# A two-layer hybrid decoder trunk: convolution inputs turned by VectorE and transfers, state space work and probability transfers placed otherwise

## Chip, core and metric

The kernel runs on one core of one Trainium2 chip. The metric is the device time of one execution in microseconds; three runs of the kernel before gave 1489.04, 1489.55 and 1492.39 us, median 1489.55 us.

## What is computed

Two layers (DEPTH 2) over 256 tokens of 1024 channels, all in float32. In each layer:

```
h += 1/2 * RMSNorm(SwiGLU(RMSNorm(h)))
h +=       RMSNorm(HybridMixer(RMSNorm(h)))
h += 1/2 * RMSNorm(SwiGLU(RMSNorm(h)))
```

The mixer, on which the change acts:

```
q, k, v, z, xbc, dt_raw, u, vg, gate_raw = split(xn @ w_in)
y_a = moba_attention(q, k, v)                  # 8 heads x 128
xbc = silu(causal_depthwise_conv(xbc, conv_w, conv_b))   # 1536 channels, 4 taps along the tokens
xs, bm, cm = split(xbc, [1024, 1280])          # 16 heads x 64; 2 groups of state 128
dt  = softplus(dt_raw + dt_bias);  a = -exp(a_log)
y_s = ssd_scan(xs, dt, a, bm, cm) + d_skip * xs          # chunks of 128 tokens
y_s = rms_norm(y_s * silu(z))
y_c = gelu(u) * (tril(sgu_w) @ layer_norm(gelu(vg)) + sgu_b)
merged = sigmoid(g0)*(y_a @ p_attn) + sigmoid(g1)*(y_s @ p_ssm) + sigmoid(g2)*(y_c @ p_sgu)
return merged @ w_out
```

With 256 tokens attention sees a single block of 256 keys, so it is causal attention with a linear distance penalty.

## The kernel before

The tokens are two tiles of 128 (t = 0, 1). All weights come as 495 blocks of 128 x 1024 float32 (512 KB), streamed in order through three rings. SyncE (SP) loads a block into `raw` (6 buffers, L160); ScalarE (ACT) rounds it into `whi` (L180), VectorE (DVE) writes the rest `wlo = raw - whi` (L181), 11 buffers each (SPLIT). Each product of the projections is three TensorE (PE) matmuls, hi x hi, hi x lo, lo x hi (L213 to L215), over 512 columns. A 512-column projection of the mixer (a chunk) is 4 blocks, so 48 matmuls for both token tiles.

The order of all work is that in which Python writes it. `gemm` walks the blocks; after each block and token tile `pump` advances a program clock by 0.65 us per three matmuls (`tick`) and lets the next block be split. Everything else is in generator tasks: `yield w` lets a task rest until the clock has gone on by `w`; the table `W` names these rests. `finish` runs tasks to their end at once, whatever they still had to rest. Each engine executes its instructions in the order written, and SP its transfers in the order issued: an instruction that waits holds up all that stands behind it on its engine.

The mixer projects in the order xbc (three chunks; the first two together), z (2), q (2), k (2), v (2), then gate and p_ssm (`br`), vg, gate and p_attn, u, gate and p_sgu, w_out. Beside them:

- `conv(c, ps)`, one task for each xbc chunk. ACT scales the projection into `xtok`, token-major (L514). PE turns it into channel-major `xc`: 8 transposes of 128 x 128 (`ctr`, L523), copied from PSUM by ACT (L526). Then ACT writes tap 3 with the bias (L545, four of 256 tokens), DVE adds taps 0 to 2 in two halves of six instructions (L551, a rest `cv` after each), ACT applies Silu (L554), and for chunks 0 and 1 PE turns the result back (`xstr`, L562) and ACT copies it into `xs` (L563). `finish(*cv)` stands behind the z projections (L952).
- `turn_whole` and `land_whole`, until now for q alone: DVE transposes each 32 x 32 square of a token tile in place (L292), 4 transfers of 64 KB for each tile write the squares to DRAM scratch `turnw` (L294), and one transfer of 512 KB brings the whole chunk back turned (L298). `turn` and `land` (L277 to L285) do the same by token tile for k, the probabilities `sc` and `y`.
- `ssd`: for t = 0, 1 and group g = 0, 1 it makes two sets of decay weights (`weights`: a PE matmul `seg` L707, DVE L709, four ACT exponentials L713, DVE L715), with a rest `w1` between and `w2` behind them; then PE multiplies them with the scaled `xs` (`yd`, L738), for t = 1 also the state with C (`yo`, L744), and DVE adds and gates (L741 to L749). `scaled(t)` writes `y = D * xs` on POOL (L695) and scales `xs` by dt on DVE (L698). After each t, `turned` transposes `y` (L277) and sends it through DRAM.
- `attention`: scores (`qk`), softmax, then DVE transposes the probabilities (L277), 8 transfers write them out, after a rest `out` two bring them back (L827), and after a rest `pv` PE multiplies them with v (L837).

Of the kernel before, what the change touches and what calls it, by code (L numbers as in the profile page):

```python
# [16 lines left out]
P = 128  # L17
L = 2
S = 256
# [25 lines left out]
ACC, TR = 5, 3  # L45


W = {'gw': 6.5, 'tr': 0, 'parts': 0, 'sq': 1.3, 'lead': 3.9, 'sq2': 5.2, 'hh': 5.2, 'x0': 0.65, 'cv': 5.2, 'cs': 6.5, 'xs': 0, 'dt1': 2.6, 'dt2': 0, 'dt3': 5.2, 'cb': 2.6, 'w1': 2.6, 'w2': 6.5, 'ys': 3.9, 'qk': 3.9, 'vv': 0, 'qs': 0, 'ex': 0, 'p1': 10.4, 'p2': 0, 'p3': 3.9, 'ge': 0, 'ln': 10.4, 'sv': 0, 'yc': 9.1, 'mg': 3.9, 'pv': 11.7, 'out': 7.8, 'in': 9.1}


@with_exitstack
def trunk(ctx, tc, a):
# [11 lines left out]
    def b4(name, shape=(P, 1024), dt=F32):  # L64
        return big.tile(list(shape), dt, name=name, tag="b4", bufs=B4)
# [49 lines left out]
    def spawn(g, wait=0):  # L115
        e = [g, wait, False]
        tasks.append(e)
        return e
# [35 lines left out]
    raws, parts = {}, {}  # L154
# [38 lines left out]
    lead = [0]  # L193
# [93 lines left out]
    def turn_whole(toks):  # L287

        rd = dram.tile([4, P, S], F32, name="turnw", tag="turnw", bufs=6)
        v = rd.rearrange("k (c i) (t a j) -> t a i (k c) j", c=4, a=4, t=NT)  # L290
        for t in range(NT):
            V.transpose(toks[t], toks[t])  # L292
            for b in range(4):
                nc.sync.dma_start(v[t, b], toks[t][32 * b:32 * b + 32, :].rearrange("p (b j) -> p b j", j=32))  # L294
        return rd
# [192 lines left out]
    def mixer(l, x, r2, nxt):  # L488
        pl = par[:, l, :]
# [28 lines left out]
        def transposed(toks, place, eng):  # L518

            for t in range(NT):  # L520
                ps = tr("ctr")
                for j in range(4):
                    T.transpose(ps[:, j * P:(j + 1) * P], toks[t][:, j * P:(j + 1) * P], ident)  # L523
                p3 = ps.rearrange("p (k t) -> p k t", k=4)
                if eng == "a":
                    A.copy(place(t), p3)  # L526
                else:
                    V.tensor_copy(place(t), p3)
                yield W["tr"]
# [5 lines left out]

        def conv(c, ps):
            toks = tokens(ps, r2, "xtok")
            xc = b4("xc", (P, 4, S))
            yield W["x0"]
            yield from transposed(toks, lambda t: xc[:, :, t * P:(t + 1) * P], "a")  # L540
            o = b4("conv", (P, 4, S))
            w = lambda j, k: pl[:, G_CW + 4 * (4 * c + j) + k:G_CW + 4 * (4 * c + j) + k + 1]
            for j in range(4):
                ct = 4 * c + j
                A.activation(o[:, j, :], xc[:, j, :], AF.Identity, scale=w(j, 3),  # L545
                             bias=pl[:, G_CB + ct:G_CB + ct + 1])
            for jj in (0, 2):
                for k in range(3):
                    s = 3 - k
                    for j in (jj, jj + 1):  # L550
                        V.scalar_tensor_tensor(o[:, j, s:], xc[:, j, :S - s], w(j, k), o[:, j, s:],  # L551
                                               op0=ALU.mult, op1=ALU.add)
                yield W["cv"]
            A.activation(o, o, AF.Silu)  # L554
            yield W["cs"]
            if c < 2:
                for t in range(NT):
                    if t not in xs:
                        xs[t] = b4(f"xs{t}")
                    pt = tr("xstr")  # L560
                    for j in range(4):
                        T.transpose(pt[:, j * P:(j + 1) * P], o[:, j, t * P:(t + 1) * P], ident)  # L562
                    A.copy(xs[t][:, 512 * c:512 * c + 512], pt)  # L563
                    yield W["xs"]
            else:
                bc["T"] = o
                pt = tr("btr")
                for g in range(SG):
                    T.transpose(pt[:, g * P:(g + 1) * P], o[:, g, 0:P], ident)
                bc["b"] = b2("btok", (P, SG * P))  # L570
                A.copy(bc["b"], pt[:, :SG * P])
# [106 lines left out]
        def ssd(ysx, rs):  # L678
# [13 lines left out]
            def scaled(t):  # L692

                y[t] = b4(f"y{t}")
                G.tensor_tensor(h3(y[t]), h3(xs[t]), hpar[:, l, 2, :, None].to_broadcast([P, SH, SP]),  # L695
                                op=ALU.mult)
                xdt[t] = xs[t]
                V.tensor_tensor(h3(xdt[t]), h3(xs[t]),  # L698
                                st["dt"][:, t * SH:(t + 1) * SH, None].to_broadcast([P, SH, SP]), op=ALU.mult)
# [19 lines left out]
            for t in range(NT):  # L719
                for g in range(SG):  # L720
                    weights(t, 2 * g)
                    if g == 0:
                        scaled(t)
                    yield W["w1"]
                    weights(t, 2 * g + 1)
                    if t == 0:

                        pst = tr("state")
                        T.matmul(pst, bc["b"][:, g * P:(g + 1) * P], xw[:, 512 * g:512 * g + 512],
                                 start=True, stop=True)  # L730
                        A.copy(state[:, 512 * g:512 * g + 512], pst)
                    yield W["w2"]
                    c = slice(512 * g, 512 * g + 512)
                    py = tr("yd")
                    for q in (2 * g, 2 * g + 1):
                        for j in range(4):
                            hh = q * 4 + j
                            T.matmul(py[:, (hh - 8 * g) * SP:(hh - 8 * g + 1) * SP], ws[t, q][:, j, :],  # L738
                                     xdt[t][:, hh * SP:(hh + 1) * SP], start=True, stop=True)
                        ws.pop((t, q))  # L740
                    V.tensor_tensor(y[t][:, c], py, y[t][:, c], op=ALU.add)  # L741
                    if t == 1:
                        po = tr("yo")
                        T.matmul(po, cT(g, 1), state[:, c], start=True, stop=True)  # L744
                        tmp = b2("yo")
                        V.tensor_tensor(h3(tmp, 8), h3(po, 8),
                                        st["eac"][:, 8 * g:8 * g + 8, None].to_broadcast([P, 8, SP]), op=ALU.mult)
                        V.tensor_tensor(y[t][:, c], y[t][:, c], tmp, op=ALU.add)
                    V.tensor_tensor(y[t][:, c], y[t][:, c], zs[t][:, c], op=ALU.mult)  # L749
                rs[t] = rsqrt([sumsq(y[t], "sy")], "rs", 1.0 / D)  # L750
                yt[t] = spawn(turned(t, y[t], pl[:, G_SSM:G_SSM + 8]), wait=1.3)


        qk = {}
# [26 lines left out]
        def attention(yax, free):  # L781
            for t in range(NT):
# [36 lines left out]
                for g in range(2):  # L819
# [2 lines left out]
                                    rden[:, None, 4 * g:4 * g + 4, None].to_broadcast([P, 4 * m, 4, 32]), op=ALU.mult)  # L822
                    rd[g] = turn(sc[g], m)
                    yield 1.3
                yield W["out"]
                for g in range(2):
                    land(sc[g].rearrange("p (m e) -> p m e", m=m), rd[g])  # L827
                yield W["pv"]
# [350 lines left out]
```

## Time and profile before

| | |
|---|---|
| median of three runs | 1489.55 us |
| the profiled execution, its own time | 1490.6 us |
| its span, first to last instruction | 1488.8 us |
| mean granted TensorE clock | 0.992 |
| busy: PE, DVE, ACT, POOL | 1461.8, 970.3, 767.7, 55.0 us |
| first matmul of xbc in layer 0 | at 193.2 us |

The two layers repeat each other: what happens in the mixer of layer 0 happens about 736 us later in layer 1 (ACT's first copy into `xs` starts at 246.52 and at 982.48). Times below are those of layer 0 in the profiled execution, in us from the span's start. A PE row's duration includes its way through the array, so rows overlap; what counts is the distance between starts, 0.227 us for a 512-column matmul at full clock.

### The profile page before, as it was taken

The page shows a single profiled execution, that of the slowest core. Times are in us where ns is not written, and L with a number is a line of the kernel's source. Part 1 is how long each engine was busy: PE and PEld are TensorE (multiplying, and loading weights), DVE is VectorE, ACT ScalarE, POOL GpSimd, SP SyncE. Part 2 cuts the span into 40 slices and gives each one's busy share as a digit, 9 for nine tenths or more (in the row PEclk, how much of TensorE's full clock was granted, in tenths as well). Part 3 has the DMA queues.
Part 4 walks back from the last instruction along what each step waited for, and adds up shares of the span by engine and source line. Part 5 has one row for each costly group of instructions (what it writes and reads, how often), then busy time and mean ns, then how long its engine had stood idle before and what let it go on. Part 6 is the DMA issues. An engine that isn't in the chain of part 4 may idle for free. (4 is left out here: it accounts for less than half of the span.)

```text
span 1488.8 us, 18560 instructions
## 1 busy us (share of the span) xinstructions
PE 1461.8 (98%) x6706; PEld 1208.7 (81%) x6706; DVE 970.3 (65%) x1188; ACT 767.7 (52%) x1051; POOL 55.0 (4%) x98
## 2 busy tenths in 40 slices
PE   9999999989989999999999999999899899999998
PEld 7888888778878888888888888888788788888886
DVE  6766477767666857666486564876776677676652
ACT  6544367455454537444364443765463635464541
POOL 0000020000000000000000000200000000000000
PEclk9999999999999999999999999999999999999999
DMA  8978555577567445878568874656774765477760
GB/s 293 332 228 263 185 191 177 161 209 224 198 213 224 172 156 197 282 243 255 154 205 268 253 251 128 221 171 187 227 230 150 230 211 169 132 261 249 262 199 28
DMA packets 151003, 312.23 MB, mean 210 GB/s; under 512 B 35456, under 2 KB 76544, under 8 KB 150912
## 3 DMA queue, kind: packets, MB, share of 16 engines
q1 hardware_dynamic: 150336, 310.73, 64.3%
q8 instruction: 52, 0.85, 0.2%
q10 hardware_dynamic: 576, 0.33, 0.1%
q14 instruction: 39, 0.32, 0.1%
HBM read 288.98 MB, written 22.02 MB: 209 GB/s over the span
## 5 line engine op out<-in xcount | busy, mean ns | idle before, releaser
L181 DVE TENSOR_TENSOR wlo<-raw,whi 128x1024 fp32r<-128x1024 f32 x495 | 593.9, 1222 | 325.9 <-ACT whi L180 323.5
L180 ACT CAST whi<-raw 128x1024 fp32r<-128x1024 f32 x495 | 511.7, 1051 | 394.8 <-PE gu L215 162.9
L213 PE MATMUL gu<-whi,xh 128*128 128x512 f32 x704 | 276.1, 392 | 1.7 <-ACT xh L328 1.3
L214 PE MATMUL gu<-wlo,xh 128*128 128x512 f32 x704 | 274.9, 391 | 0.0
L215 PE MATMUL gu<-whi,xl 128*128 128x512 f32 x704 | 274.8, 390 | 0.0
L213 PEld LDWEIGHTS gu<-whi,xh 128*128 128x128 f32 x704 | 132.6, 188 | 30.2 <-ACT xh L328 1.7
L214 PEld LDWEIGHTS gu<-wlo,xh 128*128 128x128 f32 x704 | 132.6, 188 | 28.0 <-DVE wlo L169 0.9
L215 PEld LDWEIGHTS gu<-whi,xl 128*128 128x128 f32 x704 | 132.6, 188 | 28.1 <-DVE xl L329 0.4
L213 PE MATMUL dn<-whi,hTh 128*128 128x512 f32 x352 | 137.5, 391 | 0.0
L215 PE MATMUL dn<-whi,hTl 128*128 128x512 f32 x352 | 137.0, 389 | 0.0
L214 PE MATMUL dn<-wlo,hTh 128*128 128x512 f32 x352 | 136.9, 389 | 0.0
L215 PEld LDWEIGHTS dn<-whi,hTl 128*128 128x128 f32 x352 | 66.1, 188 | 13.9
L213 PE MATMUL gate<-whi,xh 128*128 128x512 f32 x192 | 77.1, 402 | 0.0
L214 PEld LDWEIGHTS dn<-wlo,hTh 128*128 128x128 f32 x352 | 66.1, 188 | 13.6
L213 PEld LDWEIGHTS dn<-whi,hTh 128*128 128x128 f32 x352 | 66.1, 188 | 13.3
L215 PE MATMUL gate<-whi,xl 128*128 128x512 f32 x192 | 75.4, 393 | 0.0
L214 PE MATMUL gate<-wlo,xh 128*128 128x512 f32 x192 | 75.2, 392 | 0.0
L328 ACT CAST xh<-xg 128x512 fp32r<-128x512 f32 (+1 forms) x25 | 15.1, 603 | 63.0 <-DVE xg L326 63.0
L713 ACT ACTIVATE ssw<-ssw,nacs 128x128 f32<-128x128 f32 x64 | 20.5, 391 | 50.8 <-DVE ssw L709 50.8
L215 PEld LDWEIGHTS gate<-whi,xl 128*128 128x128 f32 x192 | 36.3, 189 | 7.8
L214 PEld LDWEIGHTS gate<-wlo,xh 128*128 128x128 f32 x192 | 36.4, 190 | 6.9
L213 PEld LDWEIGHTS gate<-whi,xh 128*128 128x128 f32 x192 | 36.4, 190 | 6.8
(239 smaller groups left out, 2231.3 us busy)
## 6 DMA issues: line engine op xcount, KB each, us to landing
raw<-in_mix SPq DMA_DIRECT2D x232, 512.0 KB, 4.5
raw<-in_gu SPq DMA_DIRECT2D x175, 512.0 KB, 4.9
raw<-in_dn SPq DMA_DIRECT2D x88, 512.0 KB, 4.5
turn<-hh SPq DMA_DIRECT2D x160, 64.0 KB, 1.8
hh<-turn SPq DMA_DIRECT2D x40, 256.0 KB, 5.2
row_ffn_post_g<-in_ffn_post_g SPq DMA_DIRECT2D x4, 512.0 KB, 5.7
turnw<-qtok SPq DMA_DIRECT2D x32, 64.0 KB, 2.2
qT<-turnw SPq DMA_DIRECT2D x4, 512.0 KB, 5.9
```

Of the source, the lines that this page charges most:

```text
L180: A.copy(hi, w)
L181: V.tensor_tensor(lo, w, hi.bitcast(F32), op=ALU.subtract)
L213: T.matmul(o, xh(k, t), hi[:, off:off + n], start=first, stop=False)
L214: T.matmul(o, xh(k, t), lo[:, off:off + n], start=False, stop=False)
L215: T.matmul(o, xl(k, t), hi[:, off:off + n], start=False, stop=last)
L328: A.copy(o_h, xg)
L713: A.activation(w[:, j, :], w[:, j, :], AF.Exp, bias=st["nacs"][:, c:c + 1])
```

## The change

Five edits, all in the mixer:

- `conv`: chunks 0 and 1 no longer use PE for their first turn. They rest 2.6, go through `turn_whole` (DVE, 16 transfers for both chunks), rest `out` (7.8), are brought back by `land_whole` into `xc`, rest `in` (9.1), and go on as before. Chunk 2 (B and C) keeps PE.
- `ssd`: `scaled(1)` is written in the work of t = 0, g = 1 and no longer in that of t = 1, g = 0.
- the turn of `y` of t = 0 starts 6.5 behind the end of its work, not 1.3.
- `attention`: the rest ahead of the transfers that bring the probabilities back is a new key `so`, 3.9, where it was `out`, 7.8.
- the rest `pv` behind it is 13.0, where it was 11.7.

```diff
-W = {..., 'mg': 3.9, 'pv': 11.7, 'out': 7.8, 'in': 9.1}
+W = {..., 'mg': 3.9, 'so': 3.9, 'pv': 13.0, 'out': 7.8, 'in': 9.1}
...
         def conv(c, ps):
             toks = tokens(ps, r2, "xtok")
-            xc = b4("xc", (P, 4, S))
-            yield W["x0"]
-            yield from transposed(toks, lambda t: xc[:, :, t * P:(t + 1) * P], "a")
+            if c < 2:
+                yield 2.6
+                rd = turn_whole(toks)
+                yield W["out"]
+                xc = b4("xc", (P, 4, S))
+                land_whole(xc, rd)
+                yield W["in"]
+            else:
+                xc = b4("xc", (P, 4, S))
+                yield W["x0"]
+                yield from transposed(toks, lambda t: xc[:, :, t * P:(t + 1) * P], "a")
...
                 for g in range(SG):
                     weights(t, 2 * g)
-                    if g == 0:
-                        scaled(t)
+                    if t == 0:
+                        scaled(g)
                     yield W["w1"]
...
-                yt[t] = spawn(turned(t, y[t], pl[:, G_SSM:G_SSM + 8]), wait=1.3)
+                yt[t] = spawn(turned(t, y[t], pl[:, G_SSM:G_SSM + 8]), wait=1.3 if t else 6.5)
...
-                yield W["out"]
+                yield W["so"]
                 for g in range(2):
                     land(sc[g].rearrange("p (m e) -> p m e", m=m), rd[g])
                 yield W["pv"]
```

Because the program clock orders everything, these edits move other instructions too. The lines of the changed kernel behind `conv` are 8 higher (L545 there is L553, L562 is L570). Three places follow, all in layer 0; layer 1 has the same.

The first place is ACT from the end of the first z chunk to the end of the second. `zs` is Silu of z, `xc`, `conv` and `xs` are those of the convolution. Before:

```order
L526 COPY xc<-ctr 128x4x128 x2
L545 ACTIVATE conv<-xc,par 128x256 x8
L180 CAST whi<-raw 128x1024 x3
...
L554 ACTIVATE conv<-conv 128x1024 x2
L180 CAST whi<-raw 128x1024 x2
L655 ACTIVATE zs_2135<-z,r_1662 128x512
L655 ACTIVATE zs_2137<-z,r_1739 128x512
L180 CAST whi<-raw 128x1024
L563 COPY xs_2164<-xstr 128x512 x2
```

Now:

```order
L663 ACTIVATE zs_2099<-z,r_1662 128x512
L663 ACTIVATE zs_2101<-z,r_1739 128x512
L553 ACTIVATE conv<-xc,par 128x256 x8
L180 CAST whi<-raw 128x1024 x2
L562 ACTIVATE conv<-conv 128x1024
L180 CAST whi<-raw 128x1024 x2
L562 ACTIVATE conv<-conv 128x1024
L571 COPY xs_2206<-xstr 128x512
L571 COPY xs_2213<-xstr 128x512
L562 ACTIVATE conv<-conv 128x1024
L571 COPY xs_2206<-xstr 128x512
```

The eight tap instructions of chunks 0 and 1 stood a chunk and a half ahead of `zs`; now they stand behind it, and the first of the three Silus is chunk 2's. On DVE the order behind them is: six taps of chunk 0, six of chunk 1, three `wlo`, six of chunk 0, six of chunk 1. On PE the sixteen `xstr` transposes, which stood in two groups inside the second z chunk, now stand behind its last matmul:

```order
L213 MATMUL z<-whi,xh_1682 128x512
L214 MATMUL z<-wlo,xh_1682 128x512
L215 MATMUL z<-whi,xl_1683 128x512
L570 MATMUL xstr<-con,conv 128x128 x16
L577 MATMUL btr<-con,conv 128x128 x2
L213 MATMUL q<-whi,xh_1595 128x512
```

so the q projection stands behind all of them.

The second place is DVE in `ssd`, from the gating of t = 0, g = 1 to the second set of weights of t = 1, g = 0 (`seg` are the exponents' sums, `ssw` the weights, `xs` the state space input that `scaled` multiplies). Before:

```order
L749 TENSOR_TENSOR y_2468<-y_2468,zs_2135 128x512
L709 TENSOR_TENSOR ssw<-seg,con 128x512
L715 TENSOR_TENSOR ssw<-ssw,cbt 128x512
L698 TENSOR_TENSOR xs_2189<-xs_2189,dt 128x1024
L277 STREAM_TRANSPOSE qtok<-qtok 128x512 x2
L277 STREAM_TRANSPOSE y_2468<-y_2468 128x1024
L181 TENSOR_TENSOR wlo<-raw,whi 128x1024
L709 TENSOR_TENSOR ssw<-seg,con 128x512
L715 TENSOR_TENSOR ssw<-ssw,cbt 128x512
```

Now:

```order
L757 TENSOR_TENSOR y_2468<-y_2468,zs_2099 128x512
L717 TENSOR_TENSOR ssw<-seg,con 128x512
L723 TENSOR_TENSOR ssw<-ssw,cbt 128x512
L277 STREAM_TRANSPOSE qtok<-qtok 128x512 x2
L181 TENSOR_TENSOR wlo<-raw,whi 128x1024
L717 TENSOR_TENSOR ssw<-seg,con 128x512
L723 TENSOR_TENSOR ssw<-ssw,cbt 128x512
L181 TENSOR_TENSOR wlo<-raw,whi 128x1024 x2
L277 STREAM_TRANSPOSE y_2468<-y_2468 128x1024
```

Two instructions have left the stretch between the two sets of weights: L698 stands a set of weights earlier (in t = 0, g = 1), the transpose of `y` stands behind the second set.

The third place is SP around the probabilities (`sc`) of t = 1, in one piece of the difference:

```order
 L280 DMA turn_128_3532<-sc 32x8x128 x4
 L280 DMA turn_128_3545<-sc 32x8x128 x4
-L160 DMA raw<-in_mix 128x1024 x4
+L160 DMA raw<-in_mix 128x1024 x2
 L285 DMA sc<-turn_128_3532 128x2x512
 L285 DMA sc<-turn_128_3545 128x2x512
-L160 DMA raw<-in_mix 128x1024 x17
+L160 DMA raw<-in_mix 128x1024 x19
```

Two weight loads instead of four stand between writing the probabilities out and bringing them back. On PE the `pv` matmuls of both token tiles stand 18 projection matmuls earlier than before.

## Rows read from the trace of the kernel before

**Rows 1.** The page: from its first part busy time, share of the span and number of instructions of each engine; from its list of groups the cast of the weights on ACT (count, busy us, mean ns of one, idle time ahead and its releaser).

```profile
PE 1461.8 (98%) x6706; PEld 1208.7 (81%) x6706; DVE 970.3 (65%) x1188; ACT 767.7 (52%) x1051; POOL 55.0 (4%) x98
...
L180 ACT CAST whi<-raw 128x1024 fp32r<-128x1024 f32 x495 | 511.7, 1051 | 394.8 <-PE gu L215 162.9
```

**Rows 2.** What PE itself waited for over the whole span, longest first: engine, line and tile, the releaser; us in total, times, longest us.

```profile
PE pv L837 <- DMA sc<-turn: 9.1, 2, 4.6
PE yd L738 <- DVE ssw L715: 7.7, 2, 3.8
```

**Rows 3.** The timeline of PE, from the turn of xbc to the start of q: start, us, engine, line, operation, out<-in, shape, count.

```profile
218.66 1.03 PE L523 MATMUL ctr<-con,xtok 128*128 128x128 f32 x8
...
219.45 0.48 PE L213 MATMUL xbc<-whi,xh 128*128 128x512 f32 x1
...
228.60 0.39 PE L213 MATMUL z<-whi,xh 128*128 128x512 f32 x1
...
252.92 0.39 PE L215 MATMUL z<-whi,xl 128*128 128x512 f32 x1
...
253.28 0.48 PE L213 MATMUL q<-whi,xh 128*128 128x512 f32 x1
```

**Rows 4.** The timeline of ACT in the same stretch; in brackets idle time ahead and its releaser.

```profile
216.35 2.42 ACT L514 ACTIVATE xtok<-xbc,r 128x512 f32<-128x512 f32 x4
...
222.50 4.05 ACT L545 ACTIVATE conv<-xc,par 128x256 f32<-128x256 f32 x8
...
237.34 2.00 ACT L554 ACTIVATE conv<-conv 128x1024 f32<-128x1024 f32 x2
...
241.61 1.25 ACT L655 ACTIVATE zs<-z,r 128x512 f32<-128x512 f32 x2
...
246.52 1.07 ACT L563 COPY xs<-xstr 128x512 f32<-128x512 f32 x2 [2.10 <-PE xstr L562]
```

**Rows 5.** The timeline of DVE in the same stretch.

```profile
221.65 1.22 DVE L181 TENSOR_TENSOR wlo<-raw,whi 128x1024 fp32r<-128x1024 f32 x1 [0.69 <-ACT whi L180]
...
231.38 4.82 DVE L551 SCALAR_TENSOR_TENSOR conv<-xc,par,conv 128x253 f32<-128x253 f32 x12
...
239.61 3.49 DVE L181 TENSOR_TENSOR wlo<-raw,whi 128x1024 fp32r<-128x1024 f32 x3
```

**Rows 6.** The way through DRAM as q takes it: the timeline of DVE and of SP's queue at q's first chunk, then from the page's list of transfers (count, KB each, median us from issue to landing) the weight loads and q's two kinds.

```profile
274.92 1.30 DVE L292 STREAM_TRANSPOSE qtok<-qtok 128x512 f32<-128x512 f32 x2
...
275.65 4.39 SPq L294 DMA_DIRECT2D turnw<-qtok  x8
...
raw<-in_mix SPq DMA_DIRECT2D x232, 512.0 KB, 4.5
...
turnw<-qtok SPq DMA_DIRECT2D x32, 64.0 KB, 2.2
qT<-turnw SPq DMA_DIRECT2D x4, 512.0 KB, 5.9
```

**Rows 7.** The timeline of DVE in `ssd`, between the two sets of weights of t = 1, g = 0, and the last set of t = 1, g = 1.

```profile
310.00 1.26 DVE L715 TENSOR_TENSOR ssw<-ssw,cbt 128x512 f32<-128x512 f32 x1 [1.35 <-ACT ssw L713]
311.19 1.21 DVE L698 TENSOR_TENSOR xs<-xs,dt 128x1024 f32<-128x1024 f32 x1
312.32 1.30 DVE L277 STREAM_TRANSPOSE qtok<-qtok 128x512 f32<-128x512 f32 x2
313.54 1.20 DVE L277 STREAM_TRANSPOSE y<-y 128x1024 f32<-128x1024 f32 x1
314.67 1.18 DVE L181 TENSOR_TENSOR wlo<-raw,whi 128x1024 fp32r<-128x1024 f32 x1
315.77 0.68 DVE L709 TENSOR_TENSOR ssw<-seg,con 128x512 f32<-128x512 f32 x1
317.79 0.69 DVE L715 TENSOR_TENSOR ssw<-ssw,cbt 128x512 f32<-128x512 f32 x1 [1.34 <-ACT ssw L713]
...
332.55 0.69 DVE L715 TENSOR_TENSOR ssw<-ssw,cbt 128x512 f32<-128x512 f32 x1 [1.35 <-ACT ssw L713]
```

**Rows 8.** The timeline of PE in `ssd`, t = 1: the `yd` matmuls of g = 0 in two parts, the first projection matmul behind them, the `yd` of g = 1 and the first projection matmul behind those.

```profile
313.71 1.00 PE L738 MATMUL yd<-xs,ssw 128*128 128x64 f32 x8
...
318.54 1.30 PE L738 MATMUL yd<-xs,ssw 128*128 128x64 f32 x8 [3.83 <-DVE ssw L715]
...
321.88 0.63 PE L213 MATMUL v<-whi,xh 128*128 128x512 f32 x1
...
333.43 1.89 PE L738 MATMUL yd<-xs,ssw 128*128 128x64 f32 x16
...
335.67 0.80 PE L213 MATMUL v<-whi,xh 128*128 128x512 f32 x1
```

**Rows 9.** The 2 us from 319 on: from:to, us, busy time of PE, PEld, DVE, ACT, POOL, the granted clock of TensorE, the busy share of the DMA engines and GB/s.

```profile
319.00:321.00 2.00, 2.00 (x9) 1.42 (x8) 2.00 (x2) 2.00 (x4) 0.00 (x0) 0.58 1.07 202
```

**Rows 10.** The probabilities of t = 1: the timelines of PE, DVE and SP's queue.

```profile
432.60 3.75 PE L837 MATMUL pv<-sc,v 128*128 128x128 f32 x16 [4.42 <-DMA sc<-turn]
...
422.25 4.63 DVE L181 TENSOR_TENSOR wlo<-raw,whi 128x1024 fp32r<-128x1024 f32 x4 [0.25 <-ACT whi L180]
...
418.34 7.77 SPq L160 DMA_DIRECT2D raw<-in_mix  x4
426.22 0.93 SPq L285 DMA_DIRECT2D sc<-turn  x2
```

More of the change, by code (lines that the diff above doesn't have):

```diff
@@ L45 @@
 ACC, TR = 5, 3
-W = {'gw': 6.5, 'tr': 0, 'parts': 0, 'sq': 1.3, 'lead': 3.9, 'sq2': 5.2, 'hh': 5.2, 'x0': 0.65, 'cv': 5.2, 'cs': 6.5, 'xs': 0, 'dt1': 2.6, 'dt2': 0, 'dt3': 5.2, 'cb': 2.6, 'w1': 2.6, 'w2': 6.5, 'ys': 3.9, 'qk': 3.9, 'vv': 0, 'qs': 0, 'ex': 0, 'p1': 10.4, 'p2': 0, 'p3': 3.9, 'ge': 0, 'ln': 10.4, 'sv': 0, 'yc': 9.1, 'mg': 3.9, 'pv': 11.7, 'out': 7.8, 'in': 9.1}
+W = {'gw': 6.5, 'tr': 0, 'parts': 0, 'sq': 1.3, 'lead': 3.9, 'sq2': 5.2, 'hh': 5.2, 'x0': 0.65, 'cv': 5.2, 'cs': 6.5, 'xs': 0, 'dt1': 2.6, 'dt2': 0, 'dt3': 5.2, 'cb': 2.6, 'w1': 2.6, 'w2': 6.5, 'ys': 3.9, 'qk': 3.9, 'vv': 0, 'qs': 0, 'ex': 0, 'p1': 10.4, 'p2': 0, 'p3': 3.9, 'ge': 0, 'ln': 10.4, 'sv': 0, 'yc': 9.1, 'mg': 3.9, 'so': 3.9, 'pv': 13.0, 'out': 7.8, 'in': 9.1}
 @with_exitstack
```

## The prediction

> **What bounds the kernel.** I read the busy times first: PE is busy 98% of the span [rows 1], so the time is PE's work plus PE's waits. Then PE's own waits: two places are worth a name, the `yd` matmuls, which wait for VectorE's decay weights, and the `pv` matmuls, which wait for the probabilities' way back from DRAM; each occurs once in each layer, 7.7 and 9.1 us in all [rows 2]. Then the timelines around each edit, for what ends last there. No other engine is near its limit over the span, so an edit counts only where PE has to wait for it, or where it takes an instruction off PE. All times are layer 0's; layer 1 repeats them, so each term is doubled at the end. About 0.2%, 3 us, is what a measurement of this kernel can tell from no change.
>
> **Term 1, PE's transposes (gain).** Eight `ctr` transposes start at 218.66 and the next matmul at 219.45, 0.79 us on, and that one holds PE 0.08 us longer than the usual 0.227: 0.88 us for eight [rows 3]. Sixteen leave: 1.76 us. The first z matmul then starts at 228.60 - 1.76 = 226.84. The sixteen `xstr` move behind z, so the last z matmul (252.92 before) is over at about 253.15 - 1.76 - 1.75 = 249.65.
>
> The Trainium skill prices this otherwise: "TensorE: Matmul & The Clock Gate", section "Part 4: PE-mode transpose", gives some 275 ns for one transpose in a kernel's context, by which sixteen would be worth 4.4 us. The trace does not agree as to what they displace: eight of them hold the next matmul up by 0.88 us.
>
> **Term 2, the convolution's chain (loss).** The transposes that leave PE were cheap, and what replaces them is late. Follow the new order.
>
> Transfers: `xtok` is done at 218.77 [rows 4]. DVE transposes four tiles at 1.30 for two [rows 6] behind two `wlo`, of which the second (221.65, 1.22 long [rows 5]) comes some 0.7 earlier without ACT's copies between: done at about 224.8. SP then needs 4.39 for eight writes, so 8.8 for sixteen, from about 222.8 to 231.6; +2.2 to land: 233.8 [rows 6]. A return of 512 KB lands in 5.9 [rows 6]: 239.7 for chunk 0. The second is issued behind it; it lands between 0.4 (SP's issue) and 5.9 later, 240.1 to 245.6.
>
> ACT: the taps L553 stand behind both `zs`. Those start at 241.61 - 1.76 = 239.85 and take 1.25 [rows 4], so chunk 0's taps start at 241.1 even though its input may be there sooner; eight take 4.05: chunk 1's start at 243.1, all end at 245.15. Two `whi`, 1.05 each [rows 1], 2.0 as a pair, to 247.15, Silu of chunk 2 (two in 2.00 [rows 4]) to 248.15, the next `whi` to 249.15.
>
> DVE: six taps take 2.41 (twelve in 4.82 [rows 5]). Chunk 0 from 241.7 to 244.1, chunk 1 to 246.5; three `wlo` (3.49 for three [rows 5]), whose third waits for the `whi` that ends at 249.15: 250.4. Then chunk 0's second half to 252.8, chunk 1's to 255.2.
>
> PE: Silu of chunk 0 ends at 253.9, and PE, finished with z at 249.65, stands still for 4.3 us. First eight `xstr`, ACT's two copies (1.07 [rows 4]), Silu of chunk 1 to 256.55, eight more `xstr` and two `btr`: q starts at 257.6, where it started at 253.28 [rows 3]. So the chain costs **4.3 us net of term 1**. A further price comes behind a standstill: after the 3.83 us wait for `yd` the granted clock was 0.58 over the two microseconds from 319 on [rows 9], between the chip's two levels, 1.2 and 2.4 GHz. 4.3 is longer than 3.83, so I count the `xstr` at half clock, 0.8 us each eight, of which the first eight's half delays the copies: 1.1. Taken: **+5.4**. Ends: +4.3 (clock stays up) and +8.2 (transfers 2.8 late, because three weight loads stand ahead of the returns on SP, at 4.5 each when alone [rows 6]).
>
> What hides the rest: DVE's 2.6 us of transposes fall where it has idle time, and SP's 8.8 us delay weight loads that are up to eleven blocks of 12 matmuls, 2.7 us each, ahead of PE; without that lead it would be up to 8.8. ACT stands still ahead of its taps under the same cover.
>
> **Term 3, the state space work (gain).** Before, DVE does between the two sets of weights of t = 1, g = 0: L698 1.21, two transposes of k, the transpose of `y` 1.20, one `wlo` [rows 7]. PE has its first `yd` done at 314.7 and waits to 318.54 [rows 8]. Without L698 (1.13 from start to start) and `y` (1.13), and with the first L715 no longer stretched to 1.26 from 0.69 (POOL's L695, which ran in that moment, goes with L698), DVE would be 2.8 earlier; L698 now stands one set of weights earlier, where DVE has up to 1.4 idle, and leaves 0.4 of its 1.2 behind. So PE waits to about 316.15: 1.45 instead of 3.83, too short for what happened to the clock. Before, the row of work from 318.54 to the next projection matmul at 321.88 took 3.34; at full clock it is 1.7 (g = 1 took 2.24 for both halves of `yd` and `yo` [rows 8], less 0.85 for one half, plus 0.3 for a score matmul). The projection would go on at 317.85, 4.0 earlier.
>
> But not all of it is kept. PE then reaches the last `yd` at 317.85 + 11.1 = 328.95, its second half at 329.8. The weights for that were ready at 333.24 before (L715 at 332.55 [rows 7]). DVE's chain to there is 2.3 earlier at its start, takes in the moved transpose of `y` (1.2), and fills 0.8 of its waits for ACT with it: 331.35. So a new wait of 1.5 us arises at the last `yd`, and the next projection matmul starts at 331.35 + 1.4 = 332.75, where it started at 335.67: **-2.9**, taken -2.8. Ends: -5.4 (no wait left at either `yd`) and 0 (all given back at the last one).
>
> The later turn of y of t = 0 has nothing behind it before the p_ssm projection: nothing. On SP its return stands behind two weight loads and ahead of the second k; k's lead there covers it.
>
> **Term 4, the probabilities.** At t = 0 nothing waited before, and the returns are issued two loads sooner against 4.1 us (18 matmuls) less on PE: nothing, at worst +1. At t = 1 PE comes 4.1 us earlier, at 424.1 instead of 428.2 (432.60 - 4.42 [rows 10]). SP: of the four loads (from 418.34 to 426.11) the first goes at once and the second needs the first of the four `wlo` that start at 422.25, over at 423.4 [rows 10]; with two loads ahead the returns are issued at about 423.8, not 426.22. The first `pv` followed its return's issue by 6.4 before, with three loads just ahead of it; q's single return takes 5.9 and a weight load 4.5 [rows 6], so I take 5.0 with one load ahead: 428.8. PE waits 4.7 where it waited 4.4. The end of the stage moves by +0.3, and DVE's chain ahead is a little shorter, since one cast there no longer stands behind a wait for PE. Taken: **0**, ends -1 and +1.7.
>
> **Sum.** +5.4 - 2.8 + 0 = +2.6 a layer, +5.2 for two. Against the profiled execution's own 1490.6 us (its span is 1488.8) that is 1495.8; that execution is 1.05 above the median, so the median should come to **1494.8 us**.
>
> **Rivals.**
> 1. The transfers are the late part, not the chain (18%). For it: 16 writes of 128-byte pieces and three loads ahead of the returns; against it: ACT is not ready before 241.1. At +8.2 a layer: +5.4 x 2 = +10.8, 1500.4; with `pv` at +1.7 too, 1503.8.
> 2. The terms cancel (25%): term 2 at its lower end, 4.3, and term 3 at -4.3 because the last `yd` loses little: 1489.6. If instead the transposes were worth their whole rows, which the trace speaks against, term 1 would gain 2.6 more a layer: 1489.6 as well. The second way has 4 of the 25. The price in the Trainium skill's "TensorE: Matmul & The Clock Gate", section "Part 4: PE-mode transpose", comes to the same time.
> 3. Faster (15%): moving L698 and `y` off DVE clears both `yd` waits with their half clock, -5.4 in layer 0 and no less in layer 1, against term 2 at 4.3 with the clock up: -1.1 a layer, and with `pv` at its -1 end, since the same two microseconds bring DVE's softmax forward, -2.1: 1485.4. It decides at the last `yd` of t = 1: the weights must be there by 329.8. Against it: two microseconds of DVE work are moved there, not removed.
>
> The forecast itself, slower by 3 to 9 us, has 42%. So faster 0.15, same 0.25, slower 0.60. The range, 1486 to 1504, reaches from rival 3's better half to rival 1's worse end; the forecast's own is 1492.5 to 1498.5.
>
> **What would show it.** In the changed profile: PE waits at `xstr` for ACT's Silu, about 4 us and then 1 to 2 us, in both layers, with the granted clock at half behind it; q starts 4 to 6 us later relative to the first xbc matmul. The taps L553 of chunk 0 start right behind `zs`: if they start later and wait for the transfer, rival 1 is at work. The 3.8 us waits at `yd` fall to some 1.5, and a new one stands at the last `yd`. `pv` still waits some 4 to 5 us. No wait at `xstr`, or one under 2 us, would make the prediction wrong; so would a `pv` wait that is gone.

## The result

The changed kernel takes 1505.67 us in the median (1503.93 to 1507.45, four runs) where the kernel before, run beside it, takes 1489.78: a ratio of **1.0104, interval 1.0092 to 1.0116**, by that ratio 15.5 us slower. Forecast were 1494.8 us, range 1486 to 1504. The profiled execution is the slowest of the four (1507.45 us); it has a span of 1505.6 us (1488.8 before) and a mean granted clock of 0.988 (0.992 before, 0.989 to 0.991 in the other three). The direction was right, the size a third of what came.

### The profile page after: what moved, and what is told of

It reads as the page before. It is cut to its first block, busy times and chain, and to the rows that moved or that the text cites. A ratio compares the mean times of both kernels' runs of the same rounds, so it can differ in the third digit from the quotient of the medians.

```text
span 1505.6 us, 18548 instructions
## 1 busy us (share of the span) xinstructions
PE 1465.2 (97%) x6674; PEld 1209.5 (80%) x6674; DVE 972.4 (65%) x1196; ACT 765.1 (51%) x1043; POOL 55.7 (4%) x98
## 4 chain that ended last, share of the span: by engine, by line
PE 79%; DVE 11%; ACT 4%; issue 3%; DMA 2%; POOL 0%; SPq 0%; DVEq 0%; ACTq 0%; POOLq 0%
PE gu L213 10%; PE gu L214 10%; PE gu L215 10%; PE dn L213 5%; PE dn L215 5%; PE dn L214 5%; DVE wlo L181 5%; PE br L213 3%; PE br L215 3%; PE br L214 3%; PE xbc L213 1%; PE xbc L215 1%; PE xbc L214 1%; ACT whi L180 1%; DVE conv L559 1%
```

## The profile after

The waits of PE over the span, columns as in [rows 2]:

```profile
PE xstr L570 <- ACT conv L562: 14.3, 4, 5.5
PE pv L845 <- DMA sc<-turn: 8.2, 2, 4.1
PE yd L746 <- DVE ssw L723: 4.6, 4, 1.4
PE br L213 <- ACT ysh L682: 3.1, 2, 1.6
```

Two rows are new: `xstr`, which was forecast, and `br`, which was not. Where the time went is read by following the same instructions in both traces: the start in the changed kernel minus the start before, and how it grows from one landmark to the next (us; the landmarks are the last matmul of the feed-forward layer ahead, the last of q, the first of the gate behind v, the first of vg, the first of u).

| stretch | forecast | layer 0 | layer 1 |
|---|---|---|---|
| xbc to last q: terms 1 and 2 | +5.4 | +9.27 | +9.20 |
| to the first gate: `yd`, term 3 | -2.8 | -1.29 | -2.30 |
| to vg: p_ssm | 0 | +1.95 | +2.16 |
| to u: `pv` of t = 1, term 4 | 0 | -1.72 | -0.56 |
| sum | +2.6 | +8.21 | +8.50 |

16.7 us together, of 16.8 by the spans. The convolution is more than all of it. PE there, to be held against [rows 3]:

```profile
249.24 0.39 PE L215 MATMUL z<-whi,xl 128*128 128x512 f32 x1
255.17 1.97 PE L570 MATMUL xstr<-con,conv 128*128 128x128 f32 x8 [5.54 <-ACT conv L562]
258.77 1.97 PE L570 MATMUL xstr<-con,conv 128*128 128x128 f32 x8 [1.63 <-ACT conv L562]
```

What PE waited for stands in the chain of work that ended last, followed back through this stretch (start, us, what):

```profile
238.52 0.24 PE z L215
...
238.79 1.06 ACT whi L180
...
239.88 1.22 DVE wlo L181
241.10 1.65 DVE conv L559 x5
242.75 0.24 issue
242.99 2.12 DVE conv L559 x6
...
245.36 2.12 DVE conv L559 x6
...
247.72 0.47 DVE conv L559
248.20 3.40 DVE wlo L181 x3
251.60 2.38 DVE conv L559 x6
...
254.06 1.07 ACT conv L562
...
255.17 1.98 PE xstr L570 x8
```

From 239.88 to 254.06 it is DVE: a `wlo` (whose cast on ACT had waited for PE), 18 taps, three `wlo`, six taps. No transfer is in it. ACT's taps and SP's queue in layer 0, and ACT's taps in layer 1:

```profile
240.95 4.05 ACT L553 ACTIVATE conv<-xc,par 128x256 f32<-128x256 f32 x8
...
222.75 10.08 SPq L294 DMA_DIRECT2D turnw<-xtok  x16
232.93 1.40 SPq L160 DMA_DIRECT2D raw<-in_mix  x3
234.42 1.06 SPq L298 DMA_DIRECT2D xc<-turnw  x2
...
986.09 4.05 ACT L553 ACTIVATE conv<-xc,par 128x256 f32<-128x256 f32 x8 [0.93 <-DMA xc<-turnw]
```

In layer 0 the taps follow `zs` at once, but without a margin: their return was issued at 234.42 and took 6.5 us to land. In layer 1 they wait 0.93 us for it, and the stage is no longer for that. Behind the standstill the clock, columns as in [rows 9]:

```profile
253.00:255.00 2.00, 0.00 (x0) 0.00 (x0) 2.00 (x6) 0.94 (x1) 0.00 (x0) 0.76 0.89 332
255.00:257.00 2.00, 1.83 (x8) 1.57 (x8) 2.00 (x5) 0.70 (x2) 0.00 (x0) 0.50 0.17 70
...
261.00:263.00 2.00, 2.00 (x6) 1.61 (x6) 0.00 (x0) 1.81 (x4) 2.00 (x2) 0.50 0.00 0
263.00:265.00 2.00, 2.00 (x22) 1.65 (x22) 0.00 (x0) 0.00 (x0) 1.35 (x1) 0.68 0.00 0
```

Half clock, 1.2 GHz, holds from about 254 to 264: through both groups of `xstr` and into q.

## Experiments

All ratios are to the kernel before, run beside; "stage" is the first row of the table above, measured in that run's trace.

**The edit alone, and all but it.** `e_conv_only` has the other four edits undone, `e_no_conv` the block `if c < 2` of `conv`.

> The kernel before with the convolution edit alone (chunks 0 and 1 turned by VectorE and transfers, nothing else changed). Theory: the loss is the chain behind this edit and needs none of the others. The two waits at xstr (5.5 and 1.6 us in the changed kernel) stand in both layers, TensorE runs at half clock behind them, and the steady part of q is 9.2 us later a layer, against the 5.4 that were predicted: 1489.8 + 18.5 = 1508.3 us (1506.5 to 1510). Rival: the other four edits add to it by crowding DVE, ACT or the transfers, and alone the edit costs the 5.4 a layer of the prediction: 1500.6 us.

Measured: 1508.37 us, ratio 1.0115 (1.0099 to 1.0130); stage +9.35 and +9.19; `xstr` waits 14.4 us in all. The loss is this edit's and needs none of the others.

> The changed kernel with the convolution edit undone (all chunks turned by PE again); the other four edits stay. Theory: these are worth what the stages of the changed trace show: -1.3 and -2.3 us at yd in the two layers, +1.95 and +2.15 us from a wait of 1.55 us of the p_ssm projection for y, -1.6 and -0.5 at pv: -1.6 in all, 1488.2 us (1486.5 to 1489.5), and the wait for y stands there with no convolution edit. Rival: the wait for y only comes of the delay that the convolution puts into DVE and ACT; then it is gone here and the time is 1484 to 1485 us, which is also what the prediction's terms 3 and 4 give (-5.6).

Measured: 1488.15, ratio 0.9981 (0.9971 to 0.9990): by the ratio the other four edits gain 2.8 us, where 5.6 were forecast. The new wait of `br` stands there, 3.1 in all, so it does not come from the convolution. The `yd` stretch is worth -2.20 and -3.25 here.

**Two chains.** `e_cv2` moves six taps of chunk 2 out of chunk 0's way.

```diff
-                yield W["cv"]
+                yield W["cv"] if c < 2 else (0.65 if jj == 0 else 2 * W["cv"] - 0.65)
```

> The changed kernel with one rest moved: chunk 2's second six taps follow 0.65 behind its first six, not 5.2, and its Silu stays where it was. Nothing of PE, ACT or the transfers moves; on DVE six taps (2.4 us) go from behind the third of three wlo to behind the first, where DVE had 1.5 us idle. Theory: the step of term 2 that failed is that these six taps stand ahead of chunk 0's on DVE. Without them there, Silu of chunk 0 starts at about 252.7 instead of 254.06, the first wait at xstr is 4.2 instead of 5.5, q comes 1.35 to 1.5 earlier a layer: 1505.7 - 2.9 = 1502.8 us (1501.5 to 1503.7). Rival: the convolution's inputs come late through DRAM, and the order on DVE doesn't matter: waits and time unchanged, 1505.7.

Measured: 1504.53, ratio 1.0083 (1.0070 to 1.0097), over the theory's range. Only layer 1 gained: stage +9.29 in layer 0, +6.86 in layer 1. ACT's taps in the two layers say why:

```profile
242.40 4.05 ACT L553 ACTIVATE conv<-xc,par 128x256 f32<-128x256 f32 x8 [1.38 <-DMA xc<-turnw]
...
985.12 4.06 ACT L553 ACTIVATE conv<-xc,par 128x256 f32<-128x256 f32 x8 [0.17 <-DMA xc<-turnw]
```

With DVE's chain shorter, the return is next. In layer 0 it landed at 242.38, where it had landed at 240.93 in the changed kernel, though this edit doesn't touch it. In `e_conv_only` it landed as late (242.83), and there DVE's 18 taps hid it: the first wait at `xstr` was 5.55 us. So I tried to bring the returns forward, from behind three weight loads:

```diff
-                yield W["out"]
+                yield 1.3
...
-                yield W["in"]
+                yield 17.55
```

> The run e_cv2 with its two returns of the convolution's inputs issued right behind the 16 writes, ahead of the three weight loads that stood between; the rest behind them is longer by as much, so that DVE, ACT and PE keep e_cv2's order. In e_cv2 chunk 0's taps on ACT waited 1.38 us for the return in layer 0 and 0.17 in layer 1, and only layer 1 gained. Theory: two chains end nearly together at chunk 0's Silu, the six taps of chunk 2 on DVE and the return through DRAM; with both shortened, the taps L553 wait for no transfer, Silu of chunk 0 starts at about 252.7 in both layers, the first wait at xstr is 4.2, and q comes 1.4 us earlier a layer than in the changed kernel, a little more with the half clock: 1502.3 us (1501 to 1503.3). Rival: the returns are as late as before, because they wait for the last write and not for the loads: layer 0's wait at L553 stays over 1 us and the time is that of e_cv2, 1503.3 to 1504.5.

Measured: 1508.97, ratio 1.0119 (1.0105 to 1.0133), stage +9.85 and +9.74. Both theories missed it. The returns landed in 4.3 us instead of 7.6 (medians), but the weight loads now stood behind them, and ACT's cast of such a block stands ahead of `zs` and the taps:

```profile
242.55 1.05 ACT L180 CAST whi<-raw 128x1024 fp32r<-128x1024 f32 x1 [3.96 <-DMA raw<-in_mix]
243.51 1.26 ACT L663 ACTIVATE zs<-z,r 128x512 f32<-128x512 f32 x2
244.66 4.04 ACT L553 ACTIVATE conv<-xc,par 128x256 f32<-128x256 f32 x8
```

To shorten the transfers without that, `e_half` leaves out the way through DRAM of token tile 1, and `e_half_cv2` also moves the taps.

> The changed kernel with half of the convolution's way through DRAM left out: token tile 1 of chunks 0 and 1 isn't written and brought back (its half of xc is zeros), so 8 writes of 64 KB for 16 and returns of 256 KB for 512; DVE's transposes and the order on DVE, ACT and PE stay. Theory: in the changed kernel DVE's 18 taps bind, and the transfers' lateness (0 in layer 0, 0.93 us ahead of the taps on ACT in layer 1) is hidden behind them: the inputs land 4 us earlier, no wait for a return is left, Silu of chunk 0 still starts at about 254.1, the waits at xstr stay 5.5 and 1.6 us: 1505.7 us within 1.5. Rival: the transfers set the end; then the stage is shorter by 1 us or more a layer and the time under 1503.5.

> e_half with e_cv2's order on DVE (chunk 2's second six taps behind its first six). Theory: with the transfers out of the way the move of the six taps is worth its 1.4 us in both layers, not in one: Silu of chunk 0 at 252.7, the first wait at xstr 4.1 us, q 1.4 to 2.5 us earlier a layer: 1502.3 us (1500.5 to 1503.5). Rival: something else, ACT's casts and Silu of chunk 2 or the wlo between the taps, holds chunk 0 there: no gain over e_half.

Measured: 1507.64, ratio 1.0120 (1.0106 to 1.0134; 0.4 us over the theory's range), and 1502.93, ratio 1.0085 (1.0072 to 1.0099). The stage in the four cases, layer 0 and layer 1:

| | transfers whole | transfers halved |
|---|---|---|
| taps as in the change | +9.27, +9.20 | +9.27, +8.82 |
| six taps moved | +9.29, +6.86 | +7.61, +6.60 |

Halving the transfers alone gives nothing in layer 0 and 0.4 in layer 1; with the taps moved as well the layers gain 1.7 and 2.6, and the first wait at `xstr` falls from 5.5 to 3.9 us in both. DVE's taps bind in the changed kernel, and the transfers stand right behind them.

`e_cv0` gives every chunk the short rest between its halves (0.65), so that the taps of chunks 0 and 1 have one `wlo` between them where three stood.

> The changed kernel with the rest between the two halves of every chunk's taps 0.65 instead of 5.2: on DVE the 24 taps of chunks 0 and 1 then have one wlo between their halves where three stood, chunk 2's second half stands behind its first, and the three Silus of ACT stand closer together. Transfers keep their order. Theory: with the return landing at 241 to 242.5, the chain from there to the end of the convolution (taps on ACT, 24 taps and the wlo between on DVE, Silu) sets q. Silu of chunk 0 starts at 251.7 to 252.7 instead of 254.06, that of chunk 1 at about 254.5 instead of 257.66, so q starts 3 to 4 us earlier a layer and the half clock behind is shorter: 1505.7 - 8 = 1497.5 us (1495 to 1500). Rival: the transfers set it, the taps on ACT start late and all behind them is paced by SP's queue: not under 1503.

Measured: 1502.38, ratio 1.0079 (1.0065 to 1.0093); stage +5.86 and +6.00. The stage gave 3.3 us a layer where 4 were expected; `xstr` now waits another 1.5 us a layer for ACT's copy `btok`, and ACT's taps wait 0.6 and 1.1 us for a return. The time lies between the two theories' bounds; the stage speaks for the chain, and so does Silu of chunk 0, which starts at 252.56 as expected.

**The clock.** `e_warm` puts 22 matmuls between z and `xstr`:

```diff
+        pw = tr("keep")
+        for i in range(22):
+            T.matmul(pw, x.h(i % 8, 0), x.x.hi[0][:, 0:4, :], start=True, stop=True)
         finish(*cv)
```

> The changed kernel with 22 more matmuls of 512 columns (5.0 us at full clock) between the last z matmul and xstr, into a PSUM tile that nobody reads: they fill the standstill of 5.5 us. Theory: about 3.3 us a layer of the loss is TensorE's half clock behind the standstill, which reaches through both groups of xstr and into q. Silu of chunk 0 still ends at about 255.1 and the first xstr starts there, but eight take 0.9 to 1.0 us instead of 1.97, the clock is 1.00 through q, and the time is 1505.7 - 6.6 = 1499 us (1498 to 1501). Rival: PE waits there for ACT's copies and Silu in any case, so that only the half clock in q counts (1.56 a layer): 1502.5 us. If the clock had nothing to do with it: 1505.7.

Measured: 1501.15, ratio 1.0064 (1.0050 to 1.0078): 6.0 us under the changed kernel by the ratios, 4.5 by the medians (6.6 expected); stage +5.78 and +7.24. `xstr` starts at the same moment and takes 1.09:

```profile
249.47 5.15 PE L962 MATMUL keep<-xh 128*128 128x512 f32 x22
255.18 1.09 PE L570 MATMUL xstr<-con,conv 128*128 128x128 f32 x8 [0.56 <-ACT conv L562]
257.95 1.09 PE L570 MATMUL xstr<-con,conv 128*128 128x128 f32 x8 [1.68 <-ACT conv L562]
```

In layer 0 the clock stayed at 1.00 through q. So 3.5 us of its 9.27 are clock and not wait. In layer 1 only 2.0 came back: there the clock fell behind the second wait of 1.68 (0.58 over the two microseconds from 999 on).

**y and the probabilities.** `e_no_sopv` undoes the rests `so` and `pv`; `e_yin` is `e_no_conv` with y's parts of t = 0 as early as before:

```diff
-            yield W["in"]
+            yield W["in"] if t else 3.9
             new = ysx.new(t)
```

> The changed kernel with the rests of the probabilities as before (out 7.8 ahead of the returns, pv 11.7 behind). Theory: these two rests are worth nothing, as term 4 had it: the gain at pv of t = 1 (1.6 us in layer 0) also showed with the convolution edit alone, so it is no effect of them; 1505.7 us within 1.5, pv still waits about 4 us twice. Rival: they gain what the stage shows, 1.6 and 0.5 us, and without them the time is 1507.8.

Measured: 1507.88, ratio 1.0116 (1.0103 to 1.0130), which is the rival's time and over the theory's range. The trace doesn't show the rival's effect: the stretch at `pv` gives -1.95 and -0.35, -2.30 in all, and -2.28 in the changed kernel. The two intervals overlap, and the mean granted clock of the four runs is lower (0.986 to 0.988, for 0.988 to 0.991). Whether the rests gain up to 1.8 us or nothing is not settled.

> The run e_no_conv (the convolution as before, the other edits kept) with the rest between y's return and its parts, for t = 0, 3.9 in place of 9.1: the transpose of y stays where the change put it, behind the second set of weights, and its four part instructions on DVE and two on ACT go back ahead of the transpose of y of t = 1 and of the softmax. Theory: the wait of 1.55 us of the p_ssm projection comes of those parts, which hold DVE's softmax and with it the parts of y of t = 1; it goes, with 0.4 more behind it, in both layers: e_no_conv's ratio 0.998 less 2 x 1.95 us, 1484 us against 1490.8, ratio 0.9955 (0.9945 to 0.9965). Rival: the wait comes of the other moves (scaled, the loads on SP), and the ratio stays at 0.998.

Measured: ratio 0.9982 (0.9974 to 0.9991). The wait of `br` fell from 3.1 to 0.7 in all and its stretch by 1.2 us a layer, as the theory had it, and the time did not move: the rival's ratio, but not for the rival's reason. The gain was given back by the clock. In layer 0 the stretch at `pv` lost 0.9 us (-0.78 for -1.69). In layer 1 the stretch at `yd` lost 0.95 (-2.30 for -3.25): behind a wait of 1.4 us the clock was at 0.50 from 1052 to 1054, where it had been at 1.00 in `e_no_conv`; the stretch at `pv` lost 0.2. Layer 0 at `pv` in `e_no_conv`, then in `e_yin`:

```profile
426.00:430.00 4.00, 0.81 (x7) 0.84 (x8) 2.84 (x5) 2.50 (x5) 0.00 (x0) 0.99 1.01 355
430.00:434.00 4.00, 4.00 (x17) 3.61 (x17) 3.06 (x4) 3.44 (x5) 0.00 (x0) 0.58 0.94 379
434.00:438.00 4.00, 4.00 (x27) 3.56 (x27) 2.94 (x4) 1.66 (x3) 0.00 (x0) 1.00 0.88 273
```

```profile
426.00:430.00 4.00, 2.13 (x10) 2.16 (x11) 2.26 (x4) 2.33 (x5) 0.00 (x0) 0.61 1.00 348
430.00:434.00 4.00, 4.00 (x16) 3.48 (x16) 3.64 (x5) 3.40 (x5) 0.00 (x0) 0.53 0.87 312
434.00:438.00 4.00, 4.00 (x28) 3.58 (x27) 1.83 (x3) 1.33 (x2) 0.00 (x0) 1.00 0.92 323
```

Counted at half clock (twice the share missing from 1, times 4 us), that is 3.4 us there and 6.9 here, behind waits of like length (4.16 and 3.93 us). `e_pvwarm` fills that wait with 17 matmuls of e_warm's kind, on top of `e_yin`; `e_bpv` does so in the kernel before.

> The run e_yin with 17 more matmuls of 512 columns (3.9 us) ahead of pv of t = 1, into a PSUM tile that nobody reads: they fill the wait for the probabilities (4.0 us) and no more. Theory: e_yin lost its gain at y again because the clock stood at half for 6.8 us behind both waits at pv, where e_no_conv had 3.4 us; filled, the clock stays up, pv starts no later, and 3.4 us a layer come back: ratio 0.9982 - 0.0046 = 0.9937 (0.9925 to 0.9955). Rival: the matmuls behind pv wait for other things (y_a's parts, gates), so that the clock costs little: 0.997 or more. If the filler delays pv: 0.998 or more.

> The kernel before with 17 more matmuls of 512 columns (3.9 us) ahead of pv of t = 1, into a PSUM tile that nobody reads, nothing else changed. Theory: the kernel before runs at half clock for 6.9 us in layer 0 and 3.4 in layer 1 behind its waits at pv (4.6 and 4.4 us); filled, the clock stays up and half of that comes back, 5.1 us: ratio 0.9966 (0.995 to 0.998). That would also say that the 1.6 us by which layer 0's stage at pv is shorter in the changed kernel is the clock and no effect of its rests. Rival: the clock falls all the same, because 0.5 to 0.7 us of the waits stay open, or pv comes later: ratio 0.999 or more.

Measured: `e_pvwarm` 1483.65, ratio **0.9954** (0.9941 to 0.9966), the fastest kernel here and within its theory's range; `e_bpv` 1488.76, ratio 0.9989 (0.9980 to 0.9998), over its theory's range and next to the rival's. The clock stayed at 1.00 behind `pv` in both. In `e_bpv` that stretch came 2.5 and 1.4 us earlier (3.4 and 1.7 expected) and 1.1 of it went to a wait of xbc for ACT's `xtok` in layer 1; `e_pvwarm` lost 1.7 in the same way. Against `e_yin` the stretch of `e_pvwarm` gained 2.5 and 2.3 us, 3.4 expected. `pv` itself came up to 0.4 us later. That the filled wait keeps the clock up is shown; what it gives back fell short.

**Cover for the chain.** `e_yin_late` is the changed kernel with `finish(*cv)` behind the first q projection (and y as in `e_yin`).

> The changed kernel with the same shorter rest of y, and with the end of the convolution behind the first q projection: finish(*cv) stands there, so that PE has 10.9 us of q to do while Silu and taps end. Theory: the standstill is a matter of what PE has in front of it; the waits of 5.5 and 1.6 us at xstr go with the half clock behind them, and what is left of the convolution edit is the gain of term 1, 1.76 us a layer: 1484 - 3.5 = 1480.5 us (1479 to 1484). Rival: the copies of xs stand behind three casts on ACT and right ahead of the state space sums, and Silu needs its table loaded again behind the exponential: a new wait of 1 to 4 us a layer takes the gain back, 1484 to 1489.

Measured: 1495.24, ratio 1.0031 (1.0020 to 1.0041), over both ranges. The rival's new wait came, 3.1 us a layer, and in layer 0 10 us at half clock behind it, which neither had counted:

```profile
263.69 1.47 PE L570 MATMUL xstr<-con,conv 128*128 128x128 f32 x12
268.25 1.12 PE L570 MATMUL xstr<-con,conv 128*128 128x128 f32 x4 [3.09 <-ACT xs L571]
...
264.80 2.92 ACT L180 CAST whi<-raw 128x1024 fp32r<-128x1024 f32 x3
267.62 1.55 ACT L571 COPY xs<-xstr 128x512 f32<-128x512 f32 x3
```

`e_cv0_late` adds `e_cv0`'s rests, so that the copies stand ahead of those casts.

> e_cv0's rests, with those behind the taps 2.6 and 5.2, y's shorter rest, and the end of the convolution behind the first q projection. In e_yin_late PE stood 3.1 us a layer for ACT's copies of xs, behind three casts and two more table loads, and ran at half clock for 10 us behind it; here the Silus stand ahead of the exponential of dt, the copies right behind their transposes, and the sixteen xstr inside q in two groups. Theory: the standstill was the price of having nothing on PE to cover the chain; with q's matmuls ahead no wait over 0.5 us is left at xstr, and the edit keeps term 1: 1.76 us a layer below e_yin (ratio 0.9982), 1484.3 us, ratio 0.9958 (0.994 to 0.998). Rival: the chain ends so late that xstr still waits inside q for Silu or for the copies, 2 us or more with half clock behind it: ratio 1.000 to 1.003.

Measured: ratio 1.0020 (1.0011 to 1.0029): the rival's time, but not its cause. `xstr` waits only 1.2 us a layer, for ACT's copy `dtT`, but dt's own work on DVE came later (`acsT` waits 2.1 us for it, once), and `br` waits 2.6 in all. With the filler at `pv` on top (`e_best`, 0.989 to 0.994 expected) it is 0.9989 (0.9980 to 0.9998), slower than `e_pvwarm`. No order that I tried makes the transfers pay.

## Why the prediction missed

The step that failed is the price of term 2, the convolution's chain: +5.4 us a layer were forecast, +9.27 and +9.20 measured. Two smaller steps failed beside it: y's later turn, which was put at nothing, and term 3, whose gain came to -1.29 and -2.30 for -2.8.

**Term 1 held.** The first z matmul starts at 226.74 (226.84 forecast), the last ends 0.39 behind 249.24 (249.65). Sixteen transposes were worth 1.71 us. By an estimate from the price for one transpose in the Trainium skill's "TensorE: Matmul & The Clock Gate", section "Part 4: PE-mode transpose" (some 275 ns, beside a figure for bf16; these are float32), it would have been 4.4; the trace does not agree.

**Term 2 failed, by 3.9 us a layer.** Its frame held (the taps right behind `zs`, Silu of chunk 2 first, PE idle until chunk 0's Silu, two waits), and three of its sizes did not. (a) It counted twelve taps on DVE ahead of the three `wlo`; there were eighteen, because chunk 2's second six stand behind a `wlo` whose cast is paced by PE. Silu of chunk 0 came 1.4 later than forecast, counted from the first landmark of the table; in `e_half_cv2` moving these six takes 1.6 off the wait. (b) The half clock at `xstr` was priced at 1.1 up to q; it held for both groups and `btr` and cost 2.0: q's start is another 0.9 later. (c) It went on into q and `dtps`: 1.6 more by the last q. 1.4 + 0.9 + 1.6 = 3.9. The upper end, 8.2, was built on late transfers and held the clock at the same 1.1, so it lay under the truth with the wrong cause.

**Rival 1 was nearly right about the place.** By the text's own test (do the taps wait for their transfer?) it failed in layer 0; but a return 1.5 us later is as late as DVE's chain. The prediction covered SP's writes with PE's lead in weight blocks; that held here, but e_cv2_ret shows that a late load stops ACT first, and with it `zs` and the taps. The sixteen writes took 10.08 for 8.8, and the returns 7.6 in the median to land for 5.9 [rows 6].

**Term 3 held in kind and was cut by the clock.** The waits came as forecast, 1.41 for 3.83 and a new one at the last `yd` (0.89, 1.5 forecast):

```profile
325.27 1.60 PE L746 MATMUL yd<-xs,ssw 128*128 128x64 f32 x8 [1.41 <-DVE ssw L723]
...
342.05 1.10 PE L746 MATMUL yd<-xs,ssw 128*128 128x64 f32 x8 [0.89 <-DVE ssw L723]
```

The clock behind the first of them:

```profile
326.00:328.00 2.00, 2.00 (x8) 1.45 (x7) 2.00 (x3) 2.00 (x4) 0.00 (x0) 0.50 0.65 234
```

But 1.41 us was not "too short for what happened to the clock": it stood at half again. In `e_no_conv`, with the same wait, it stayed at 1.00, and the stretch gave -2.20 and -3.25, about the -2.8 of the sum. That layer 1 gains more goes with the kernel before, where the clock was at half behind this wait for 6.8 us in layer 1 and for 3.4 in layer 0.

**That y's later turn costs nothing failed,** by +1.95 and +2.16. DVE at the softmax of t = 0, then ACT and PE at p_ssm:

```profile
358.70 0.69 DVE L683 TENSOR_TENSOR ysl<-y,ysh 128x512 fp32r<-128x512 f32 x1 [0.69 <-ACT ysh L682]
359.31 0.87 DVE L810 SCALAR_TENSOR_TENSOR sc<-con,qk 128x128 f32<-128x128 f32 x4
...
376.76 0.62 ACT L682 CAST ysh<-y 128x512 fp32r<-128x512 f32 x1 [4.97 <-DVE y L681]
...
377.43 0.50 PE L213 MATMUL br<-whi,ysh 128*128 128x512 f32 x1 [1.55 <-ACT ysh L682]
```

The parts of y of t = 0 (L681, L683) now stand right ahead of the softmax, which they hold up by 2.1 us against PE (`nmx`, its last step ahead of the exponentials, is 9.97 later than before, PE's gate 7.83); the parts of t = 1 stand behind the softmax, and `br` waits for those. I had asked who reads this y, and not what its instructions stand in front of. e_yin took most of the wait away (3.1 to 0.7) by moving only them. (The Trainium skill's "Perfetto Trace Analysis", section "Tensor Engine Instruction (MATMUL, LD_WEIGHTS)", calls ACT and DVE strict FIFO. The trace agrees: the softmax's first instruction starts at 359.31, right behind L683, though PE had written its scores by 355.4.)

**Term 4 held as far as the traces go:** `pv` waits 4.1 us (4.7 forecast), and no trace shows an effect of the rests; by `e_no_sopv`'s time up to 1.8 us stay open. The -1.72 in layer 0 goes with the clock, 6.9 us at half in the kernel before and 3.4 in the changed one; `e_conv_only`, with the old rests, has -1.69.

Not settled: why the same wait lowers the clock for 3.4 us in one kernel and 6.8 in another. It differs within one execution too: in the kernel before, 3.4 us in layer 0 and 6.8 in layer 1 behind the same 3.83 us at `yd`, and 6.8 and 3.4 behind 4.42 and 4.65 us at `pv`. So doubling layer 0's terms was right for the order of the work, not for the clock. About 2 us a layer of any comparison of these kernels hang on it.

## What to carry to other kernels

Between a late input and its consumer count every instruction that stands in the queue of each engine on the way, other chunks' halves too, and ask of the one ahead what paces it. A standstill of PE costs its length and then the clock: behind 5.5 us it took another 3.5 in layer 0, and filling the wait with matmuls that nobody reads gave them back. A step that is moved later is not free because its reader is far: look at what it now stands ahead of.

## What was not expected of the hardware

- Behind waits of 4.0 to 4.6 us at `pv` the clock was at half for 3.4 us in some kernels and about 6.8 in others; behind 1.4 us at `yd` it fell in the changed kernel and not in `e_no_conv`. The Trainium skill says in "TensorE: Matmul & The Clock Gate", section "Part 1: The HAM clock gate (the "warmup" mystery)", that the number of slow matmuls varies from run to run of one kernel; the runs agree as far as they show it: the mean granted clock of the changed kernel's four runs goes from 0.988 to 0.991. In the traces the time at half clock can't be read from the wait's length.
- Matmuls that nobody reads keep the clock up: 1.00 behind the filled waits at `pv` in both layers, ratio 0.9954 against 0.9982 without them; `pv` came 0.2 and 0.3 us later for it.
- Writes of 64 KB in pieces of 128 bytes occupied SP's queue for 0.63 us each (16 in 10.08). A return of 512 KB landed in 7.6 us in the median with three weight loads right ahead of it on SP, and in 4.3 with the loads behind it.
